# Seven block products for the gate in the up-projection of a two-layer decoder's MLP

## The chip, the cores and the metric

The kernel runs on one core of one Trainium2 chip. The metric is the device time of one execution in microseconds (us). A core has a matrix engine (TensorE, PE in the profile) that multiplies a stationary 128 x 128 block by a moving operand and adds up in PSUM banks of 128 x 512 float32; a vector engine (VectorE, DVE), a scalar engine (ScalarE, ACT), a small general engine (GpSimd, POOL) and a queue that issues transfers (SyncE, SP). Each engine takes its instructions in the order in which they were written into its own queue; engines wait for each other through semaphores.

## What is computed

The reference is a trunk of two layers over 512 positions of width 1024. Each layer has a mixer (windowed attention with a short convolution in layer 0, chunked gated linear attention in layer 1), the gated MLP, and a per-layer embedding. The change is in the MLP, which is the same in both layers:

```
def _conv_ffn(h, w_up, conv_w, conv_b, w_down):
    u = _causal_depthwise_conv(h @ w_up, conv_w) + conv_b
    gate, up = jnp.split(u, 2, axis=-1)
    return (jax.nn.gelu(gate, approximate=False) * up) @ w_down
...
x = x + _conv_ffn(_rms_norm(x, ffn_norm[i]), ffn_w_up[i], ffn_conv_w[i], ffn_conv_b[i], ffn_w_down[i])
```

`h` is 512 x 1024, `w_up` is 1024 x 5632 (2816 gate columns, then 2816 up columns), the convolution goes over three neighbouring positions in each column, and `w_down` is 2816 x 1024. All is float32.

## The kernel before

Activations lie transposed: `xT[k]`, k = 0 to 7, holds 128 features by 512 positions. Every product is made of three matmuls on split operands (`mm3`, lines 157 to 159): a value is its rounded part ("hi", type fp32r) plus the rest ("lo"), and hi x hi, hi x lo and lo x hi are added in one PSUM bank. ACT writes the hi part and DVE subtracts to get the lo part: `split` for activations (lines 101 and 102, with a gain 104 and 105) and `cut` for weights (lines 137 and 138). The RMS norm's factor R, one number per position, is multiplied in after the product (line 785), so `xg[k]` is only the split of `xT[k]` times the norm's gain.

`ffn` (from line 770) goes over 11 column groups. In group d, `weights` loads 256 gate columns and 256 up columns, 1 MB each, into two `raw` buffers (SP's queue, line 111), and cuts each into two hi/lo pairs of 128 x 1024, one per 128-column half. There are three `wh` and three `wl` buffers for these pairs. For each of the two halves PE makes a gate column and an up column, 8 x 3 = 24 matmuls each, 512 positions wide, into a `ps` bank; then `taps` does the rest: z = bank x R on DVE (785), bias and the last tap on ACT (786), the two other taps on DVE (788). The gate column gets Gelu on ACT (810), the product with the up column is formed on DVE (813) and split at once into `acts[f]` (101, 102). There are four `ps` and four `pa` banks, three `z` buffers and four `zt` buffers. The 22 pairs in `acts` are the moving operands of the down-projection, `project` (from line 349), whose three weight chunks per output pair go through the same `raw`, `wh` and `wl` buffers. In layer 1, `blocks` prepares the block sums that the embedding's gate uses, with scratch from the `zt` buffers, and `ple1` takes its transposed rows from there too (`back`).

Which instruction stands where in each queue is not the order of the source. A list scheduler places them by its own costs, except within the stretches marked `manual_schedule`, of which the MLP has none. So matmuls of different columns may be interleaved, and a cut of the next group's weights may stand before or behind the taps of the current one. A tile's buffer is handed on when its last reader is done: the instruction that writes the next tile into it waits for that reader.

Of the kernel before, what the change touches and what calls it, by code (L numbers as in the profile page):

```python
# [18 lines left out]
P = 128  # L19
S = 512  # L20
D = 1024
NT = S // P
ND = D // P
DFF = 2816
NF = DFF // P
# [3 lines left out]
ET = mybir.EngineType  # L29
LEVELS = (64, 32, 16, 8, 4, 2, 1)  # L30
CW = 512
TWO_PI = 2.0 * np.pi
PI_SAFE = 3.1415925

# [22 lines left out]
class Kernel:  # L57
# [60 lines left out]
    def cut(self, rv, by, pool=None, bufs=3):  # L118


        nc = self.nc
        pool = pool or self.wp
        na, nb = rv.shape[1:]
        parts = []
        n = 2 if na * nb > 1024 else 1
        for k in range(n):
            if by == "b":
                a, b = na, nb // n
                v = rv[:, :, k * b : (k + 1) * b]
# [7 lines left out]
            nc.scalar.activation(hv, v, AF.Copy)  # L137
            nc.vector.tensor_tensor(lv, v, hv.bitcast(F32), ALU.subtract)  # L138
# [12 lines left out]
        return get  # L151
# [178 lines left out]
    def spread(self):  # L330
# [7 lines left out]
        for i, x in enumerate((rh.bitcast(F32), rl)):  # L338
# [41 lines left out]
    def rope_tables(self, pool):  # L380
# [54 lines left out]
    def mixer0(self):  # L435
        nc, a, tc = self.nc, self.a, self.tc
        with tc.tile_pool(name="m0", bufs=1) as mp:
# [275 lines left out]
            w = conv_w("x", 0)  # L713
            R = self.spread()
            qn0 = query(0)
# [51 lines left out]
            self.end_norm()  # L767


    def ffn(self, i, next_gain):  # L770
        nc, a, tc = self.nc, self.a, self.tc
        xg, R = self.xg, None
        wu = a["ffn_w_up"][i].rearrange("(k p) n -> p k n", p=P)
        w0, w1, w2, bb = self.fcv
        with tc.tile_pool(name=f"ffn{i}", bufs=1) as fp:
            acts = [self.pair(self.fp, "b0", "b1") for f in range(8)]
            for f in range(8, NF, 2):
                four = self.four(fp)
                acts += [(four[:, 0], four[:, 1]), (four[:, 2], four[:, 3])]

            def taps(ps, f):
                y = fp.tile([P, S], F32, tag="zt", name=self.nm("zt"), bufs=4)
                z = fp.tile([P, S + 2], F32, tag="z", name=self.nm("z"), bufs=3)
                nc.gpsimd.memset(z[:, :2], 0.0)
                nc.vector.tensor_tensor(z[:, 2:], ps, R, ALU.mult)  # L785
                nc.scalar.activation(y, z[:, 2:], AF.Identity, scale=w2[:, f : f + 1], bias=bb[:, f : f + 1])  # L786
                for tap, w in ((1, w1), (0, w0)):
                    nc.vector.scalar_tensor_tensor(  # L788
                        out=y, in0=z[:, tap : tap + S], scalar=w[:, f : f + 1], in1=y, op0=ALU.mult, op1=ALU.add
                    )  # L790
                return y

            for d in range(NF // 2):
                wg = self.weights(wu[:, :, 256 * d : 256 * d + 256], ND, 256)
                wv = self.weights(wu[:, :, DFF + 256 * d : DFF + 256 * d + 256], ND, 256)
                for c in range(2):
                    f = 2 * d + c
                    got = []
                    pss = []
                    for w in (wg, wv):  # L800
                        ps = self.ps()
                        for k in range(ND):
                            self.mm3(ps, w(k, c * P, (c + 1) * P), xg[k], start=k == 0, stop=k == ND - 1)
                        pss.append(ps)
                    if R is None:
                        R = self.spread()
                    for w, ps, fo in ((wg, pss[0], f), (wv, pss[1], NF + f)):
                        y = taps(ps, fo)
                        if w is wg:
                            nc.scalar.activation(y, y, AF.Gelu)  # L810
                        got.append(y)
                    g, y = got
                    nc.vector.tensor_tensor(y, g, y, ALU.mult)  # L813
                    self.split(acts[f], y)
            self.begin_norm(("a0", "a1"))
            done = self.residual(next_gain)
            if i == 1:
                self.forms = []
                scratch = lambda: fp.tile([P, S], F32, tag="zt", name=self.nm("gx"), bufs=4)

                def done(m, ps):
                    nc.vector.tensor_tensor(self.xT[m], self.xT[m], ps, ALU.add)
                    self.blocks(m, next_gain, scratch)
# [75 lines left out]
    def ple1(self, fp):  # L899
# [49 lines left out]
        def back(hf, t):  # L949

            pb = self.pa()
            for q in range(4):
                nc.tensor.transpose(
                    pb[:, q * P : (q + 1) * P], self.xT[4 * hf + q][:, t * P : (t + 1) * P], self.ident
                )
            x = fp.tile([P, 512], F32, tag="zt", name=self.nm("xt"), bufs=4)
            nc.scalar.copy(x, pb)
            return x

# [45 lines left out]
        X, Q = [[self.ps() for _ in range(2)] for _ in range(2)]  # L1005
        both = (0, H)
        with tc.manual_schedule(engines={ET.PE, ET.DVE, ET.Activation}):
# [42 lines left out]
            halves = ((0, H // 2), (H // 2, H))  # L1050
            Y = [Q[0]] + [y[:, : H // 2] for y in (Q[1], X[0])]
# [481 lines left out]
```

## Time and profile before

| what | value |
|---|---|
| median of 3 runs | 1247.51 us (1247.4 to 1247.59) |
| the profiled execution's own time | 1248.2 us |
| its span, first to last instruction | 1246.4 us |
| PE busy | 1236.1 us, 99% of the span |
| DVE busy | 804.6 us, 65% |
| ACT busy | 561.5 us, 45% |
| POOL busy | 52.1 us, 4% |
| granted TensorE clock, mean | 1.0 |
| DMA, mean | 94 GB/s |

The profile is of one execution. Its page names instruction groups by line, engine, operation, written tile and read tiles, then size and count, then busy time and the mean duration in ns of one, then the idle time of the engine before them and what ended most of it. In a timeline each line has the start, the duration, the engine, the line in the source, and in brackets how long the engine had been idle before it and what released it. A line of `mm3`, `split` or `cut` is that of the helper; the tile names (`ps<-a,wh`) tell which product it is. Records of matmuls overlap, since the engine is pipelined.

### The profile page before, as it was taken

What the parts mean: (1) busy time and instruction counts of PE and PEld (TensorE: products, weight loads), DVE (VectorE), ACT (ScalarE), POOL (GpSimd) and SP (SyncE); (2) the same over time, 40 slices, a digit from 0 to 9 for tenths busy, and PEclk for the clock granted to TensorE, in tenths of its full rate; (3) what the DMA queues carried; (4) which work ended last, traced back from release to release, by engine and by line L of the source; (5) the groups of instructions that cost most, each with busy time, mean ns of one, the idle gap of its engine ahead of it and who ended that gap; (6) DMA issues with size and microseconds to landing.
All of it is one profiled execution on the core that took longest, in us unless ns stands there. A gap on an engine that the chain in (4) does not pass through costs nothing.

```text
span 1246.4 us, 15216 instructions
## 1 busy us (share of the span) xinstructions
PE 1236.1 (99%) x5984; PEld 1023.9 (82%) x5984; DVE 804.6 (65%) x1251; ACT 561.5 (45%) x873; POOL 52.1 (4%) x152
## 2 busy tenths in 40 slices
PE   9999999999999999999999999999999999999998
PEld 8877788888888888888987878888888888888887
DVE  6886556777777633346679875557777777444495
ACT  7466344444444322234563554335444444333374
POOL 2500000000000000000100000000000000000000
PEclk9999999999999999999999999999999999999999
DMA  6222232233333232223322222332223333322411
GB/s 214 92 80 56 83 102 83 88 100 102 101 102 101 83 103 93 93 74 103 111 91 68 69 68 68 101 110 95 83 94 102 101 101 102 101 93 94 149 46 68
DMA packets 111004, 117.45 MB, mean 94 GB/s; under 512 B 2728, under 2 KB 106210, under 8 KB 110932
## 3 DMA queue, kind: packets, MB, share of 16 engines
q1 hardware_dynamic: 109568, 115.35, 28.4%
q8 instruction: 47, 0.77, 0.2%
q0 software_dynamic: 560, 0.42, 0.2%
q10 hardware_dynamic: 804, 0.70, 0.2%
q14 instruction: 25, 0.20, 0.0%
HBM read 114.37 MB, written 2.10 MB: 93 GB/s over the span
## 4 chain that ended last, share of the span: by engine, by line
PE 88%; DVE 7%; ACT 2%; issue 1%; POOL 1%; DVEq 0%; ACTq 0%; POOLq 0%
PE ps L157 26%; PE ps L158 26%; PE ps L159 26%; DVE wl L138 1%; PE ps L947 1%; PE ps L946 1%; PE ps L945 1%; PE pa L1367 1%; PE pa L1344 0%; PE pa L595 0%; PE pa L158 0%; PE pa L192 0%; PE pa L159 0%; DVE F L1228 0%; PE pa L157 0%
## 5 line engine op out<-in xcount | busy, mean ns | idle before, releaser
L137 ACT ACTIVATE wh<-raw 128x1024 fp32r<-128x1024 f32 (+4 forms) x212 | 214.2, 1012 | 333.3 <-PE ps L158 298.7
L138 DVE TENSOR_TENSOR wl<-raw,wh 128x1024 fp32r<-128x1024 f32 (+4 forms) x212 | 246.5, 1164 | 153.2 <-ACT wh L137 152.1
L157 PE MATMUL ps<-a,wh 128*128 128x512 f32 x864 | 336.9, 390 | 0.0
L158 PE MATMUL ps<-a,wh 128*128 128x512 f32 x864 | 336.6, 390 | 0.0
L159 PE MATMUL ps<-a,wl 128*128 128x512 f32 x864 | 336.3, 389 | 0.0
L158 PEld LDWEIGHTS ps<-a,wh 128*128 128x128 f32 x864 | 162.3, 188 | 34.0 <-issue 0.3
L159 PEld LDWEIGHTS ps<-a,wl 128*128 128x128 f32 x864 | 162.2, 188 | 33.9
L157 PEld LDWEIGHTS ps<-a,wh 128*128 128x128 f32 x864 | 162.2, 188 | 33.7 <-issue 0.7
L788 DVE SCALAR_TENSOR_TENSOR zt<-z,vfa,zt 128x512 f32<-128x512 f32 x176 | 131.3, 749 | 3.6 <-ACT zt L786 0.6
L157 PE MATMUL ps<-b,wh 128*128 128x512 f32 x320 | 126.0, 395 | 0.5 <-ACT b L101 0.5
L159 PE MATMUL ps<-b,wl 128*128 128x512 f32 x320 | 125.7, 393 | 0.0
L158 PE MATMUL ps<-b,wh 128*128 128x512 f32 x320 | 125.0, 391 | 0.0
L785 DVE TENSOR_TENSOR z<-ps,R 128x512 f32<-128x512 f32 x88 | 60.3, 687 | 74.7 <-PE ps L159 74.7
L157 PE MATMUL ps<-four,wh 128*128 128x512 f32 x224 | 87.1, 389 | 0.0
L158 PE MATMUL ps<-four,wh 128*128 128x512 f32 x224 | 87.1, 389 | 0.0
L159 PE MATMUL ps<-four,wl 128*128 128x512 f32 x224 | 87.1, 389 | 0.0
L786 ACT ACTIVATE zt<-z,vfb 128x512 f32<-128x512 f32 x88 | 70.9, 808 | 5.0 <-DVE z L785 3.3
L157 PEld LDWEIGHTS ps<-b,wh 128*128 128x128 f32 x320 | 60.0, 188 | 14.0 <-ACT b L101 1.3
L159 PEld LDWEIGHTS ps<-b,wl 128*128 128x128 f32 x320 | 60.1, 188 | 12.5
L158 PEld LDWEIGHTS ps<-b,wh 128*128 128x128 f32 x320 | 60.1, 188 | 12.5
L810 ACT ACTIVATE zt<-zt 128x512 f32<-128x512 f32 x44 | 27.8, 631 | 74.9 <-DVE zt L788 74.8
L101 ACT ACTIVATE four<-zt 128x512 fp32r<-128x512 f32 x28 | 17.7, 632 | 77.3 <-DVE zt L813 77.3
(359 smaller groups left out, 1555.0 us busy)
## 6 DMA issues: line engine op xcount, KB each, us to landing
raw<-in_ffn_w_up_dram SPq DMA_DIRECT2D x44, 1024.0 KB, 5.1
raw<-in_ffn_w_down_dram SPq DMA_DIRECT2D x16, 1024.0 KB, 4.7
raw<-in_hy_w_in_dram SPq DMA_DIRECT2D x8, 1024.0 KB, 5.0
raw<-in_gla_w_in_dram SPq DMA_DIRECT2D x8, 1024.0 KB, 5.3
raw<-in_ffn_w_down_dram SPq DMA_DIRECT2D x8, 768.0 KB, 4.1
raw<-in_ple_w_gate_dram SPq DMA_DIRECT2D x6, 1024.0 KB, 4.7
raw<-in_gla_w_out_dram SPq DMA_DIRECT2D x4, 1024.0 KB, 4.8
raw<-in_gla_w_in_dram SPq DMA_DIRECT2D x4, 672.0 KB, 4.0
```

The costliest lines, as they stand in the source:

```text
L101: nc.scalar.activation(h, src, AF.Copy)
L137: nc.scalar.activation(hv, v, AF.Copy)
L138: nc.vector.tensor_tensor(lv, v, hv.bitcast(F32), ALU.subtract)
L157: mm(out, lh, rh, start=start, stop=False)
L158: mm(out, lh, rl, start=False, stop=False)
L159: mm(out, ll, rh, start=False, stop=stop)
L785: nc.vector.tensor_tensor(z[:, 2:], ps, R, ALU.mult)
L786: nc.scalar.activation(y, z[:, 2:], AF.Identity, scale=w2[:, f : f + 1], bias=bb[:, f : f + 1])
L788: nc.vector.scalar_tensor_tensor(out=y, in0=z[:, tap : tap + S], scalar=w[:, f : f + 1], in1=y, op0=ALU.mult, op1=ALU.add)
L810: nc.scalar.activation(y, y, AF.Gelu)
L945: mm(o, lh, rh, start=first and j == 0, stop=False, **kw)
L946: mm(o, lh, rl, start=False, stop=False, **kw)
```

## The change

The activations and weights of a gate group are seen as 2 x 2 blocks: positions left and right (two halves of 256), feature blocks even and odd (`xT[2j]`, `xT[2j+1]`), and columns first and second (two halves of 128). Of the eight block products of such a scheme, seven suffice with sums and differences of blocks (Winograd's form of Strassen's scheme). This is done for the gate in groups d = 2 to 9 of each layer (`SEVEN`); the up columns, and groups 0, 1 and 10, are made as before.

- `sums` makes, from `xT` in groups 0 and 1, the four activation sums of each pair j (four operations of 256 on DVE, two gains on ACT) and splits them (two splits of 512). They lie in the eight `b0`/`b1` pairs, which held the first eight pairs of `acts` before.
- `seven` cuts the first blocks' weights as they are (`w1`), then forms weight differences in place in the `raw` buffer and cuts them: `w13`, `w2` (in the `sq` buffers) and `w4`. It makes seven products of 12 matmuls, 256 positions wide, in three banks W, X and Y; five copies on ACT carry partial results from one half bank to another, and one of them keeps the fourth result, `more`, in SBUF, which `taps` adds to the second column on DVE.
- In the seven-product groups the order in the source is: load of the gate's `raw`, load and cut of the up columns (`wv`), `seven`, `taps` of both gate columns, one Gelu over both (128 x 1024), and then the two up columns, in `pa` banks.
- Results of a group are multiplied in one 128 x 1024 operation and kept unsplit in `kept`; the splits into `acts` come later: the first eight in group 9, the others, two at a time, after the loop in the source.
- `zt` becomes two buffers of 2 x 512 in place of four of 512; `back` in `ple1` and `blocks` take halves of these.

```diff
+    def sums(self, j, gain, scratch):
...
+        for u in range(2):
+            nc.scalar.activation(scratch[:, u], self.xT[2 * j + u], AF.Copy, scale=gain[:, 2 * j + u : 2 * j + u + 1])
+        e, o, s12, s34 = (scratch[:, u] for u in range(4))
+        out = []
+        nc.vector.tensor_tensor(s12[:, :H], e[:, H:], o[:, H:], ALU.add)
+        nc.vector.tensor_tensor(s12[:, H:], s12[:, :H], e[:, :H], ALU.subtract)
+        nc.vector.tensor_tensor(s34[:, :H], e[:, :H], e[:, H:], ALU.subtract)
+        nc.vector.tensor_tensor(s34[:, H:], o[:, :H], s12[:, H:], ALU.subtract)
+        for x in (s12, s34):
+            hl = self.pair(self.fp, "b0", "b1")
+            self.split(hl, x)
...
+    def seven(self, raw, xg, forms):
...
+        W = self.pa()
+        X, Y = self.ps(), self.ps()
+        rv = raw.rearrange("p (j u) n -> p j u n", u=2)
+
+        def cut(src, wide=True):
+
+            if wide:
+                h, l = (self.wp.tile([P, 1024], F32R, tag=g, name=self.nm(g), bufs=3) for g in ("wh", "wl"))
+            else:
+                h, l = (self.sp.tile([P, S], F32R, tag="sq", name=self.nm("t2"), bufs=2) for _ in range(2))
...
+            nc.scalar.activation(h, src, AF.Copy)
+            nc.vector.tensor_tensor(l, src, h.bitcast(F32), ALU.subtract)
...
+        def product(out, w, c, x, first=False):
+            kw = dict(skip_group_check=True)
+            for j in range(ND // 2):
+                (wh, wl), (xh, xl) = w(j, c), x(j)
+                mm(out, wh, xh, start=first and j == 0, stop=False, **kw)
+                mm(out, wh, xl, start=False, stop=False, **kw)
+                mm(out, wl, xh, start=False, stop=j == ND // 2 - 1, **kw)
...
+        w1 = cut(raw[:, :, :P])
+
+        nc.vector.tensor_tensor(b11, b12, b11, ALU.subtract)
+        nc.vector.tensor_tensor(b12, b22, b12, ALU.subtract)
+        w13 = cut(rv[:, :, 0])
+        nc.vector.tensor_tensor(b11, b22, b11, ALU.subtract)
+        w2 = cut(b11, False)
+        nc.vector.tensor_tensor(b21, b21, b11, ALU.subtract)
+        w4 = cut(rv[:, :, 1])
+        product(W[:, left], w1, 0, plain(0, 0), True)
+        nc.scalar.copy(Y[:, left], W[:, left])
+        nc.scalar.copy(X[:, left], W[:, left])
+        product(W[:, right], w13, 0, s1, True)
+        more = self.sp.tile([P, S], F32, tag="acc", name=self.nm("more"), bufs=1)[:, :H]
+        nc.scalar.copy(more, W[:, right])
+        product(Y[:, left], w2, 0, s2)
+        nc.scalar.copy(X[:, right], Y[:, left])
+        product(X[:, left], w1, 1, plain(1, 0))
+        product(X[:, right], w13, 1, s3)
+        nc.scalar.copy(Y[:, right], X[:, right])
+        product(Y[:, left], w4, 1, s4)
+        product(X[:, right], w4, 0, plain(1, 1))
+        return X, Y, more
...
             for d in range(NF // 2):
...
+                g, y = both(), both()
+                cg, cv = 256 * d, DFF + 256 * d
+                if SEVEN[0] <= d < SEVEN[1]:
+                    raw = self.raw(ND, 256)
+                    nc.sync.dma_start(raw, wu[:, :, cg : cg + 256])
+                    wv = self.weights(wu[:, :, cv : cv + 256], ND, 256)
+                    X, Y, more = self.seven(raw, xg, forms)
+                    taps(g[:, 0], X, 2 * d)
+                    taps(g[:, 1], Y, 2 * d + 1, more)
+                    nc.scalar.activation(g, g, AF.Gelu)
+                    for c in range(2):
+                        taps(y[:, c], columns(wv, c, self.pa), NF + 2 * d + c)
+                else:
...
+                nc.vector.tensor_tensor(u, g, y, ALU.mult)
+                if d < 2:
+                    for j in (2 * d, 2 * d + 1):
+                        forms.append(self.sums(j, gain, scratch[j]))
+                if d == SEVEN[1] - 1:
+                    for f in range(8):
+                        hl = self.pair(self.fp, "b0", "b1")
+                        self.split(hl, at(f))
+                        acts.append(hl)
+            for d in range(4, NF // 2):
+                split_pair(y if d == NF // 2 - 1 else kept[d // 2][:, 2 * (d % 2) : 2 * (d % 2) + 2])
```

In the text below, Y left, X right and so on are half banks, a product's number is its place in `seven`, w1, w13, w2, w4 are the cuts above, wv0 and wv1 the two cuts of the up columns, and "bias operation" is the ACT step of `taps` (line 786 before).

More of the change, by code (lines that the diff above doesn't have):

```diff
@@ L31 @@
 CW = 512
+SEVEN = (2, 10)
 TWO_PI = 2.0 * np.pi
@@ L767, in mixer0 @@
             self.end_norm()
+    def sums(self, j, gain, scratch):
+        nc = self.nc
+        H = S // 2
+        for u in range(2):
[9 more added lines that the diff above has]
+            self.split(hl, x)
+            for c in (slice(0, H), slice(H, S)):
+                out.append((hl[0][:, c], hl[1][:, c]))
+        return out
@@ new lines, in seven, with plain @@
+    def seven(self, raw, xg, forms):
+        nc = self.nc
+        H = S // 2
+        mm = nc.tensor.matmul
+        W = self.pa()
[6 more added lines that the diff above has]
+                h, l = (self.sp.tile([P, S], F32R, tag="sq", name=self.nm("t2"), bufs=2) for _ in range(2))
+            h, l = (x.rearrange("p (j n) -> p j n", n=src.shape[2]) for x in (h, l))
+            nc.scalar.activation(h, src, AF.Copy)
+            nc.vector.tensor_tensor(l, src, h.bitcast(F32), ALU.subtract)
+            h, l = (x.rearrange("p j n -> p (j n)").rearrange("p (k n) -> p k n", n=P) for x in (h, l))
+            return lambda j, c: (h[:, (2 * j if wide else j) + c, :], l[:, (2 * j if wide else j) + c, :])
+        def product(out, w, c, x, first=False):
[5 more added lines that the diff above has]
+                mm(out, wl, xh, start=False, stop=j == ND // 2 - 1, **kw)
+        def plain(u, half):
+            c = slice(half * H, (half + 1) * H)
+            return lambda j: (xg[2 * j + u][0][:, c], xg[2 * j + u][1][:, c])
+        s1, s2, s3, s4 = (lambda j, q=q: forms[j][q] for q in range(4))
+        b11, b12, b21, b22 = (rv[:, :, u, c * P : (c + 1) * P] for u in range(2) for c in range(2))
+        left, right = slice(0, H), slice(H, S)
+        w1 = cut(raw[:, :, :P])
[20 more added lines that the diff above has]
+        return X, Y, more
@@ L772, in ffn @@
         xg, R = self.xg, None
+        gain = self.g_ffn[i]
         wu = a["ffn_w_up"][i].rearrange("(k p) n -> p k n", p=P)
@@ L775, in ffn, with both, taps @@
         with tc.tile_pool(name=f"ffn{i}", bufs=1) as fp:
[L776 to L782, printed above, removed]
+            forms, kept, acts = [], [], []
+            def both():
+                return fp.tile([P, 2, S], F32, tag="zt", name=self.nm("zt"), bufs=2)
+            def taps(y, ps, f, more=None):
                 z = fp.tile([P, S + 2], F32, tag="z", name=self.nm("z"), bufs=3)
                 nc.gpsimd.memset(z[:, :2], 0.0)
-                nc.vector.tensor_tensor(z[:, 2:], ps, R, ALU.mult)
+                if more is None:
+                    nc.vector.tensor_tensor(z[:, 2:], ps, R, ALU.mult)
+                else:
+                    h2 = lambda x: x.rearrange("p (u t) -> p u t", u=2)
+                    nc.vector.tensor_tensor(
+                        h2(z[:, 2:]), h2(ps), more.unsqueeze(1).to_broadcast([P, 2, S // 2]), ALU.add
+                    )
+                    nc.vector.tensor_tensor(z[:, 2:], z[:, 2:], R, ALU.mult)
                 nc.scalar.activation(y, z[:, 2:], AF.Identity, scale=w2[:, f : f + 1], bias=bb[:, f : f + 1])
@@ L790, in taps, with columns @@
                     )
-                return y
-            for d in range(NF // 2):
[L794 to L814, printed above, removed]
+            def columns(w, c, bank):
+                ps = bank()
+                for k in range(ND):
+                    self.mm3(ps, w(k, c * P, (c + 1) * P), xg[k], start=k == 0, stop=k == ND - 1)
+                return ps
@@ new lines, in place, with split_pair, at @@
+            def place(d):
+                if d == NF // 2 - 1:
+                    return None
+                if d % 2 == 0:
+                    kept.append(self.four(fp, F32))
+                return kept[d // 2][:, 2 * (d % 2) : 2 * (d % 2) + 2]
+            def split_pair(x):
+                four = self.four(fp)
+                self.split((four[:, :2], four[:, 2:]), x)
+                acts.extend([(four[:, u], four[:, 2 + u]) for u in range(2)])
+            def at(f):
+                return kept[f // 4][:, f % 4]
@@ new lines, in ffn @@
+            scratch = [self.four(fp, F32) for _ in range(ND // 2)]
+            for d in range(NF // 2):
+                g, y = both(), both()
[10 more added lines that the diff above has]
+                        taps(y[:, c], columns(wv, c, self.pa), NF + 2 * d + c)
+                else:
+                    wg = self.weights(wu[:, :, cg : cg + 256], ND, 256)
+                    wv = self.weights(wu[:, :, cv : cv + 256], ND, 256)
+                    for c in range(2):
+                        pss = [columns(w, c, self.ps) for w in (wg, wv)]
+                        if R is None:
+                            R = self.spread()
+                        taps(g[:, c], pss[0], 2 * d + c)
+                        nc.scalar.activation(g[:, c], g[:, c], AF.Gelu)
+                        taps(y[:, c], pss[1], NF + 2 * d + c)
+                u = place(d)
+                if u is None:
+                    u = y
+                nc.vector.tensor_tensor(u, g, y, ALU.mult)
[7 more added lines that the diff above has]
+                        acts.append(hl)
@@ L818, in ffn, with half @@
                 self.forms = []
-                scratch = lambda: fp.tile([P, S], F32, tag="zt", name=self.nm("gx"), bufs=4)
+                halves = []
+                def half():
+                    if not halves:
+                        x = both()
+                        halves.extend([x[:, 0], x[:, 1]])
+                    return halves.pop(0)
+                self.half = half
                 def done(m, ps):
                     nc.vector.tensor_tensor(self.xT[m], self.xT[m], ps, ALU.add)
-                    self.blocks(m, next_gain, scratch)
+                    self.blocks(m, next_gain, half)
             self.project(self.rows(a["ffn_w_down"][i]), acts, ND, done)
@@ L955, in back @@
                 )
-            x = fp.tile([P, 512], F32, tag="zt", name=self.nm("xt"), bufs=4)
+            x = self.half()
             nc.scalar.copy(x, pb)
```

## The prediction

> **What bounds the kernel now.** First the page's busy table and the costliest groups: TensorE (PE) is busy for 99% of the span, and nearly all of that is `mm3`.
>
> ```profile
> PE 1236.1 (99%) x5984; PEld 1023.9 (82%) x5984; DVE 804.6 (65%) x1251; ACT 561.5 (45%) x873; POOL 52.1 (4%) x152
> L157 PE MATMUL ps<-a,wh 128*128 128x512 f32 x864 | 336.9, 390 | 0.0
> L138 DVE TENSOR_TENSOR wl<-raw,wh 128x1024 fp32r<-128x1024 f32 (+4 forms) x212 | 246.5, 1164 | 153.2 <-ACT wh L137 152.1
> L788 DVE SCALAR_TENSOR_TENSOR zt<-z,vfa,zt 128x512 f32<-128x512 f32 x176 | 131.3, 749 | 3.6 <-ACT zt L786 0.6
> L810 ACT ACTIVATE zt<-zt 128x512 f32<-128x512 f32 x44 | 27.8, 631 | 74.9 <-DVE zt L788 74.8
> raw<-in_ffn_w_up_dram SPq DMA_DIRECT2D x44, 1024.0 KB, 5.1
> ```
>
> A mean of 390 ns is a pipelined record, not a price. The price of a matmul is the distance between starts, so I read the timeline of PE twice: 512 wide in a projection, and 256 wide in the key/value product at the start.
>
> ```profile
> 1.32 3.35 PE L192 MATMUL pa<-ones_r 128*128 128x512 f32 x7 [1.32 <-DVE mhalf L181]
> ...
> 8.78 0.28 PE L158 MATMUL pa<-wl,a 128*128 128x256 f32 x1
> 8.90 0.28 PE L159 MATMUL pa<-wh,a 128*128 128x256 f32 x1
> 9.02 0.28 PE L157 MATMUL pa<-wh,a 128*128 128x256 f32 x1
> ...
> 500.13 0.39 PE L158 MATMUL ps<-four,wh 128*128 128x512 f32 x1
> 500.36 0.39 PE L159 MATMUL ps<-four,wl 128*128 128x512 f32 x1
> 500.58 0.39 PE L157 MATMUL ps<-four,wh 128*128 128x512 f32 x1
> ```
>
> 512 columns cost 0.2267 us (three starts span 0.68), 256 columns 0.1196 (0.24 for two): more than half. The first line matters later: seven matmuls out of idle are 0.43 us apart.
>
> Last the timeline of VectorE (DVE) and ScalarE (ACT) inside the MLP, half a column group of the 21.76 us (96 x 0.2267) that one takes:
>
> ```profile
> 310.64 0.69 DVE L102 TENSOR_TENSOR four<-zt,four 128x512 fp32r<-128x512 f32 x1 [0.70 <-ACT four L101]
> 311.25 0.68 DVE L785 TENSOR_TENSOR z<-ps,R 128x512 f32<-128x512 f32 x1
> 311.93 1.23 DVE L138 TENSOR_TENSOR wl<-raw,wh 128x1024 fp32r<-128x1024 f32 x1
> 313.07 1.53 DVE L788 SCALAR_TENSOR_TENSOR zt<-z,vfa,zt 128x512 f32<-128x512 f32 x2
> 316.50 0.69 DVE L785 TENSOR_TENSOR z<-ps,R 128x512 f32<-128x512 f32 x1 [1.90 <-PE ps L159]
> ...
> 310.84 1.06 ACT L137 ACTIVATE wh<-raw 128x1024 fp32r<-128x1024 f32 x1 [0.23 <-PE ps L158]
> 311.97 0.82 ACT L786 ACTIVATE zt<-z,vfb 128x512 f32<-128x512 f32 x1
> ```
>
> Starts on DVE: 0.61 us for 512 elements from SBUF, 0.68 from PSUM, 1.14 for 1024, 0.66 to 0.77 for a tap. On ACT: 1.06 for the hi half of 1024 (0.97 to the next), 0.82 for L786. One engine answers another within 0.04 us (a hi ends at 311.90, its lo starts at 311.93). What the reader is to see: each hi/lo pair is made as soon as PE lets a buffer go. With three buffers and one used up per 24-matmul column (5.44 us), that is two columns, 10.9 us, before PE needs it, and this lead is why PE never waits here.
>
> **The change part by part.** *Matmuls.* A group's gate was 48 at 0.2267 = 10.88 us and becomes 7 x 12 = 84 at 0.1196 = 10.05. The up half stays 10.88. A group is 20.93 us of PE instead of 21.76: 0.83 saved, 16 groups: 13.3 us. That is 7.6% of the gate and not one eighth, because a 256-wide matmul costs 5.5% over half.
>
> *Work on the other engines, per group.* DVE: five lo cuts of 1024 (5.7), one of 512 (0.6), four weight differences of 512 (2.4), five z operations (3.2), eight taps (5.5), one 1024 product (1.1): 18.5 us of 20.9. By the same prices it had 15.2 (four cuts, four z, eight taps, two products, two split halves). ACT gains five half-bank copies from PSUM (`st<-pa`, 256 wide, took 0.376). Neither is full, so neither bounds by volume. The activation splits (22 hi and lo of a layer) only move.
>
> *Order, the dear part.* A group now needs five hi/lo pairs out of the same three buffers: wv0 and wv1 (up half), w1, w13, w4. I follow the three queues as the instructions of the changed kernel stand in them, one group, time 0 at the end of its seventh product, a prime for the next group.
> PE after 0: six matmuls left of the up column (to 1.36), which free wv1's buffer; then at once two of the next group's first product, which need w1' hi, and w1' gets just that buffer. So the lead is gone. On ACT, w1' hi stands behind the bias operations (L786) of both gate columns and of the first up column, the hi of wv0' and wv1', Gelu over 1024, and the bias operation of the second up column. Step by step:
> - z of gate column X on DVE 0.04 to 0.73, its bias operation on ACT to 1.60; four gate taps from 0.91, done 3.71.
> - the load of wv' is issued when w4 lo is cut (2.67 before 0) and lands 5.1 later, at 2.43; hi of wv0' and wv1' then start at 2.47 and 3.44.
> - Gelu 4.41 to about 5.5 (1.1 for 1024, from L810's 0.631 for 512 and L137's two widths).
> - z of the second up column is behind six DVE operations, 4.28 to 4.97; its bias operation waits for Gelu, 5.44 to 6.25; w1' hi 6.17 to 7.23.
> PE waits from 1.36 to 7.27: 5.91 us. It then has 2 x 0.1196 + 8 x 0.2267 = 2.05 of work, until 9.32, and needs w1' lo. DVE reaches that after lo wv0' (5.62), a tap, lo wv1' (7.42) and a tap, 9.22 to 10.45: 1.17 us more. The other handovers (w13, w2, the copies, w4) cost 0.2 together, since the planner put up-column matmuls between them. A group's period is 20.93 + 7.29 = 28.22 us. With 0.10 for each answer instead of 0.04 it is 29.1, with none 27.8.
>
> *Sum.* Seven such boundaries a layer, two layers: 14 x 7.29 = +102.1. The entry into the first of these groups, the last of them (eight splits cut into its queue) and the exit aren't of this form: entry about 1.7 (16 `sums` operations of 256 and 8 splits, 10 to 12 us of DVE, in the second group), last 1.3, exit 1.0, so 4.0 a layer, bounds 0 and 8: +8. Saved: -13.3. Together +96.8.
>
> *PE out of idle.* No gap in the trace of before is over 1.3 us, so it doesn't show what 5.9 us do. Lower bound: nothing. Upper: the nearest row is the start, where matmuls out of idle ran 0.43 apart and the batch of eight at 6.43 still took 2.40 us instead of 1.98 (7 x 0.2267 + 0.39), slow for some 5 us. Five slow microseconds after each gap first stretch the 2.05 us of work to 4.1, of which 1.17 replaces the second wait, then slow part of the next ten: +1.2 a boundary; slow until the next column too, +2.3. I take 0.9: 14 x 0.9 = +12.6.
> [...]
>
> The profiled execution took 1248.2 us (span 1246.4, the rest around it), 0.7 above the median 1247.5. 1248.2 + 96.8 + 12.6 = 1357.6, on the median's footing **1357**.
>
> **The rivals.**
> *The clock stays up.* The same waits, no slow restart: 1247.5 + 96.8 = 1344. For it: the granted clock of the first 2 us window reads 1.00, as everywhere. Against: the starts there are 0.43 apart all the same, so this column does not show such a slowness.
> *Only the buffer turn costs.* ACT would reach w1' hi as soon as PE frees the buffer: 1.06 + 0.1 of wait, lo 1.23 later under 1.8 us of cover, about 1.4 with its smaller handovers. 14 x 1.4 - 13.3 = +6: 1254. Against: both queues are in order, and seven operations stand ahead.
> *Faster.* The matmul saving is kept: 1247.5 - 13.3 = 1234. For it: PE is the bound, 99%, and DVE and ACT have room in volume. It decides where the wait per boundary is under 13.3 / 14 = 0.95 us. Against: the hi cut alone is 1.06 after the buffer comes free, with nothing for PE ahead of it.
> *DVE becomes the bound.* If strided differences and the z sum with a broadcast cost up to twice the 0.61 (at most 5 x 0.61 = 3.1 a group), DVE comes to 21.6 us a group and the late cuts move by up to 3 us: 14 x 3 = 42 on top, 1399. Against: no row has such a stride; taps with one element's offset show no penalty.
>
> **How the numbers follow.** Forecast 0.60, clock stays up 0.20, DVE dearer 0.08, only the buffer turn 0.06, faster 0.06. The first two reach, with periods of 27.8 to 29.1 (14 x -0.4 and +0.9), edges 0 to 8 a layer, and restart 0 to 2.3, from 1330 to 1397. Down to **1305** for waits one third shorter than followed (14 x 2.4 = 34 under 1344 makes 1310, and 4 less if entry, last and exit cost half), and up to **1400**. About 0.15 is left out. One measurement of this kernel tells 0.2% (2.5 us) from no change: faster 0.06, same 0.02 (the tail of the 1254 case), slower 0.92.
>
> **What would show it.** In the changed kernel's page PE's share falls to 91% or so, with waits of the first product's matmul on ACT's `wh` cut, once per group, about 6 us, fourteen times, and a shorter one on DVE's `wl`. The distance of the 256-wide starts should be 0.12. Matmuls behind the long gap should start over 0.4 (512 wide) apart for some microseconds, or the restart term is wrong. Wrong would be: gaps under 1 us at the boundaries, gaps after the second product or after the copies instead, or DVE without idle time in the eight groups.

## The result, and the profile after

| what | before | after |
|---|---|---|
| median | 1247.62 us (6 runs, 1247.4 to 1248.38) | 1364.33 us (6 runs, 1362.66 to 1366.3) |
| profiled execution, span | 1248.2 us, 1246.4 us | 1366.3 us, 1364.5 us |
| up-projection on PE, layer 0 / layer 1 | 240.84 / 240.80 us | 301.64 / 297.28 us |
| granted TensorE clock, mean | 1.0 | 0.966 |

The ratio is 1.0936, with a 95% interval from 1.0922 to 1.095: 116.7 us slower. The up-projection, read as the time from its first matmul to the first of the down-projection, lost 60.8 us in layer 0 and 56.5 in layer 1, together 117.3; so the whole loss lies in the stretch that was changed.

The changed kernel's page, busy table, costliest groups and DMA issues (all helper lines stand one line lower than before):

```profile
PE 1267.4 (93%) x6560; PEld 1058.1 (78%) x6560; DVE 888.5 (65%) x1375; ACT 617.3 (45%) x987; POOL 52.6 (4%) x152
L139 DVE TENSOR_TENSOR wl<-raw,wh 128x1024 fp32r<-128x1024 f32 (+4 forms) x180 | 206.9, 1151 | 141.4 <-ACT wh L138 141.4
L879 DVE SCALAR_TENSOR_TENSOR zt<-z,vfa,zt 128x512 f32<-128x512 f32 x176 | 124.9, 746 | 10.2 <-ACT zt L877 9.9
L818 PE MATMUL pa<-a,wh 128*128 128x256 f32 x64 | 24.8, 387 | 85.7 <-ACT wh L809 85.7
raw<-in_ffn_w_up_dram SPq DMA_DIRECT2D x44, 1024.0 KB, 5.0
```

PE now idles 85.7 us ahead of one group of 64 matmuls: L818 is the first matmul of a product, and what it waits for is the hi cut of `w1` on ACT (L809). The price of a tap (746 ns, was 749) and of a weight cut's lo half (1151 ns, was 1164) hardly changed. PE is busy for more microseconds than before (1267 against 1236) although it has less to multiply: slow matmuls count as busy.

One boundary between two seven-product groups, in the timeline of PE:

```profile
318.28 0.58 PE L818 MATMUL pa<-a,wh 128*128 128x256 f32 x1 [5.68 <-ACT wh L809]
318.65 0.42 PE L819 MATMUL pa<-a,wh 128*128 128x256 f32 x1
318.87 0.63 PE L158 MATMUL pa<-a,wh 128*128 128x512 f32 x1
319.30 0.63 PE L159 MATMUL pa<-a,wh 128*128 128x512 f32 x1
...
321.43 0.44 PE L158 MATMUL pa<-a,wh 128*128 128x512 f32 x1
321.71 0.39 PE L159 MATMUL pa<-a,wh 128*128 128x512 f32 x1
321.94 0.28 PE L820 MATMUL pa<-a,wl 128*128 128x256 f32 x1
```

The same boundary on ACT:

```profile
311.34 2.23 ACT L877 ACTIVATE zt<-z,vfb 128x512 f32<-128x512 f32 x3 [3.43 <-DVE z L876]
313.62 2.00 ACT L138 ACTIVATE wh<-raw 128x1024 fp32r<-128x1024 f32 x2
315.53 1.04 ACT L916 ACTIVATE zt<-zt 128x1024 f32<-128x1024 f32 x1
316.48 0.80 ACT L877 ACTIVATE zt<-z,vfb 128x512 f32<-128x512 f32 x1
317.18 1.04 ACT L809 ACTIVATE wh<-raw 128x1024 fp32r<-128x1024 f32 x1
```

This is the queue that the prediction followed: three bias operations, both hi cuts of wv', Gelu, a fourth bias operation, and only then `w1'`. PE had stopped at 312.60 (318.28 - 5.68), when the last up column ended; that buffer was free from then on, and ACT reached it 4.6 us later. After the gap the matmuls are 0.43 us apart, and from 321.71 on 0.23 again.

The table by stretches of the same boundary (us; busy time and instructions of PE, PEld, DVE, ACT and POOL; granted clock; DMA share; GB/s):

```profile
316.00:318.20 2.20, 0.00 (x0) 0.00 (x0) 2.20 (x4) 2.20 (x3) 0.10 (x1) 0.50 0.00 0
318.30:319.30 1.00, 1.00 (x4) 0.91 (x4) 1.00 (x2) 0.00 (x0) 0.00 (x0) 0.50 0.00 0
322.30:325.00 2.70, 2.70 (x18) 2.36 (x17) 1.78 (x3) 0.64 (x2) 0.00 (x0) 1.00 0.74 259
```

In the last 2.2 us of PE's wait DVE and ACT work without a pause: over the span they have time to spare (DVE 65%), but too much to do just here. The granted clock is already 0.50 in the gap and stays there for the first matmuls behind it.

### The profile page after: what moved, and what is told of

Same layout as the page of the kernel before. It is cut to its first block, busy times and chain, and to the rows that moved or that the text cites. A ratio compares the mean times of both kernels' runs of the same rounds, so it can differ in the third digit from the quotient of the medians.

```text
span 1364.5 us, 16685 instructions
## 1 busy us (share of the span) xinstructions
PE 1267.4 (93%) x6560; PEld 1058.1 (78%) x6560; DVE 888.5 (65%) x1375; ACT 617.3 (45%) x987; POOL 52.6 (4%) x152
## 4 chain that ended last, share of the span: by engine, by line
PE 74%; DVE 11%; ACT 9%; issue 2%; DMA 2%; POOL 1%; DVEq 0%; POOLq 0%; ACTq 0%
PE ps L158 14%; PE ps L159 14%; PE ps L160 14%; PE pa L158 5%; PE pa L159 5%; PE pa L160 4%; ACT wh L138 2%; DMA raw<-in_ffn_w_up_dram 2%; ACT zt L877 2%; PE ps L818 2%; PE pa L818 2%; PE ps L820 2%; PE ps L819 2%; ACT wh L809 2%; DVE wl L139 1%
## 5 line engine op out<-in xcount | busy, mean ns | idle before, releaser
L138 ACT ACTIVATE wh<-raw 128x1024 fp32r<-128x1024 f32 (+4 forms) x180 | 178.3, 1000 | 303.2 <-PE ps L159 253.8
L139 DVE TENSOR_TENSOR wl<-raw,wh 128x1024 fp32r<-128x1024 f32 (+4 forms) x180 | 206.9, 1151 | 141.4 <-ACT wh L138 141.4
L158 PE MATMUL ps<-a,wh 128*128 128x512 f32 x352 | 138.0, 392 | 0.9 <-ACT wh L138 0.9
L159 PE MATMUL ps<-a,wh 128*128 128x512 f32 x352 | 137.4, 390 | 0.0
L160 PE MATMUL ps<-a,wl 128*128 128x512 f32 x352 | 137.4, 390 | 0.0
L158 PE MATMUL pa<-a,wh 128*128 128x512 f32 x256 | 109.8, 429 | 0.0
L159 PE MATMUL pa<-a,wh 128*128 128x512 f32 x256 | 109.5, 428 | 0.0
L160 PE MATMUL pa<-a,wl 128*128 128x512 f32 x256 | 106.8, 417 | 0.0
L810 DVE TENSOR_TENSOR wl<-raw,wh 128x1024 fp32r<-128x1024 f32 x48 | 58.7, 1222 | 70.2 <-ACT wh L809 70.2
L818 PE MATMUL pa<-a,wh 128*128 128x256 f32 x64 | 24.8, 387 | 85.7 <-ACT wh L809 85.7
L818 PEld LDWEIGHTS pa<-a,wh 128*128 128x128 f32 x64 | 16.2, 254 | 93.6 <-ACT wh L809 92.5
L158 PEld LDWEIGHTS ps<-a,wh 128*128 128x128 f32 x352 | 66.1, 188 | 15.7 <-ACT wh L138 1.7
L809 ACT ACTIVATE wh<-raw 128x1024 fp32r<-128x1024 f32 x48 | 50.6, 1054 | 60.1 <-PE ps L819 23.5
L160 PEld LDWEIGHTS ps<-a,wl 128*128 128x128 f32 x352 | 66.1, 188 | 14.5 <-DVE wl L139 0.8
```

The costliest lines, as they stand in the source:

```text
L158: mm(out, lh, rh, start=start, stop=False)
L159: mm(out, lh, rl, start=False, stop=False)
L160: mm(out, ll, rh, start=False, stop=stop)
L809: nc.scalar.activation(h, src, AF.Copy)
L810: nc.vector.tensor_tensor(l, src, h.bitcast(F32), ALU.subtract)
L818: mm(out, wh, xh, start=first and j == 0, stop=False, **kw)
```

## The experiments

All medians stand beside runs of the kernel before on the same chip; ratios are to those, with 95% intervals.

| run | what it is | us | ratio |
|---|---|---|---|
| late_split | only the late splits, no seven-product group | 1250.05 | 1.0017 [1.0008, 1.0026] |
| one_group | one seven-product group per layer | 1254.51 | 1.0052 [1.0037, 1.0067] |
| warm | filler matmuls in the gap | 1360.94 | 1.0905 [1.0889, 1.0922] |
| prep_first | next group's loads and w1 cut ahead of the taps | 1325.62 | 1.0621 [1.0603, 1.0639] |
| own_w1 | own buffer for the w1 pair | 1338.36 | 1.0727 [1.0711, 1.0743] |
| own_prep | both of these | 1256.68 | 1.0071 [1.0056, 1.0086] |
| roomy | and own raw buffers for the up columns | 1252.41 | 1.0033 [1.002, 1.0045] |
| edges | and both ends of the stretch prepared ahead | 1253.03 | 1.0045 [1.0031, 1.0059] |
| lazy | and the last splits where they are first needed | 1243.78 | 0.9968 [0.9956, 0.998] |

**Is it the boundaries, or the rest of the change?** Two kernels take boundaries out and leave the rest.

```diff
-SEVEN = (2, 10)
+SEVEN = (10, 10)      (late_split)
+SEVEN = (9, 10)       (one_group)
```

> No group is made with seven products; the activation sums are still formed in groups 0 and 1 (their results go unused), the activations are split late and zt is two wide buffers, as in the changed kernel. Theory (the loss sits in the handover of weight buffers between seven-product groups): at most the entry, sums and late splits, 1247 to 1256 us. Rival (late splitting or the sums carry a good part of the 117 us): 1275 us or more.

> Only group 9 of each layer is made with seven products, so there is no boundary between two of them. Theory: entry and exit only, 2 x (1.5 to 5) less 2 x 0.83, 1249 to 1257 us. Rival (each seven-product group costs by itself, through its products, copies or differences, 117 / 16 = 7.3 us): 1247.6 + late_split's loss + 14.6, about 1265 us.

late_split came 2.1 us over before (1250.05 against 1247.96): the moved splits, the block sums, the wider product and the new buffers cost nearly nothing alone. One group per layer, which has an entry and an exit but no boundary between two such groups, adds 4.5 us. So some 110 of the 117 us belong to the boundaries.

**How dear is the slow restart?** The same kernel, with 22 matmuls on a tile of ones in each boundary's gap, so that PE never stops for long; the order of the other work is held.

```diff
+        if after is not None:
+            rhs = self.ones_r.unsqueeze(1).to_broadcast([P, NT, P])
+            with self.tc.issue_after(after.ins):
+                for _ in range(22):
+                    mm(W, self.ones_r, rhs, start=True, stop=True, skip_group_check=True)
```

> All queues stand as in the changed kernel, with 22 matmuls of ones (512 wide, result overwritten) added on PE in each of the 14 long waits, about 5.0 of the 5.4 to 6.9 us, so that PE never idles long. Theory: the granted clock stays at 1.0, matmuls behind the wait are 0.227 apart at once, the wait for w1' lo of about 1.2 us shows itself, and a boundary gets some 1.0 us shorter: 1350 us (1342 to 1356). If the slow restart were worth all of the 2.3 us by which the matmuls behind a gap are late: 1332. If the clock did not matter: 1364.

It came out at 1360.94: only 3.4 us less than after where 14 were expected (1350), and above the expected range. The waits of PE in it, two boundaries:

```profile
348.36 0.39 PE L818 MATMUL pa<-a,wh 128*128 128x256 f32 x1 [0.53 <-ACT wh L809]
351.94 0.39 PE L822 MATMUL pa<-a,wl 128*128 128x256 f32 x1 [1.24 <-DVE wl L810]
377.15 0.39 PE L818 MATMUL pa<-a,wh 128*128 128x256 f32 x1 [0.53 <-ACT wh L809]
380.74 0.39 PE L822 MATMUL pa<-a,wl 128*128 128x256 f32 x1 [1.24 <-DVE wl L810]
```

With matmuls at full speed (0.39 records) the second wait, on the lo cut of `w1'`, is there as forecast: 1.24 us (forecast 1.17). In after the slow matmuls cover it. Boundaries 2 to 7, from one group's first matmul to the next one's, take 174.20 us in layer 0 and 173.20 in layer 1; in after they take 181.46 and 176.68. That is 1.21 and 0.58 us per boundary, 0.9 on the mean, the forecast's term. The total gained less because the first boundary is longer in warm, 31.1 us against 27.6, in each layer: in after the planner had put 18 up-column matmuls where the order held here allows 8, and in warm PE waits 1.92 us there for the lo cut, and 512-wide matmuls soon behind it start 0.43 us apart (236.23 to 238.79 in layer 0). The experiment was therefore not as clean as meant; the comparison of boundaries 2 to 7 is the part that answers. It bundles everything that the filler changed there, the late loads (below) too: in layer 0 ACT waits for four of them in after and for two in warm, in layer 1 for none in after and one in warm. So layer 1's 0.58 is nearer to the clock alone than layer 0's 1.21, and that the mean is just 0.9 is partly luck.

**Place in the queue, or buffer?** prep_first changes the place alone, own_w1 the buffer alone, own_prep both.

```diff
+                    raw, wv, first = ready or prep(d)                       (prep_first, own_prep)
+                    X, Y, more = self.seven(raw, xg, forms, first)
+                    pss = [columns(wv, c, self.pa) for c in range(2)]
+                    ready = prep(d + 1) if d + 1 < SEVEN[1] else None
...
-                h, l = (self.wp.tile([P, 1024], F32R, tag=g, name=self.nm(g), bufs=3) for g in ("wh", "wl"))
+                four = self.four(fp)                                        (own_w1, own_prep; w1 only)
+                h, l = (four[:, 2 * u : 2 * u + 2].rearrange("p a b -> p (a b)") for u in range(2))
```

`prep(d)` issues the loads of group d and traces the cuts of `w1` and of the up columns; it now stands ahead of the taps and Gelu of group d - 1.

> The same work with the same buffers as the changed kernel; only the source order differs: loads and first cut (w1) of the next group are traced ahead of the taps of this one, the first cut ahead of the up cuts. In the queues w1' now stands before the sixth product and the up cuts behind three taps. [...] Rival (the seven products or their volume on DVE are what costs): over 1340 us.

> The changed kernel in its own source order, but the hi/lo pair of a group's first weight block (w1) gets a buffer of its own, so that it no longer takes the buffer which up column c1 frees last. Theory (the place in the queue ties the cut, the buffer is only the second tie): with the buffer free, the planner can put the w1' cut ahead of the taps in some boundaries, and in these the long wait is gone and a shorter one, on the hi of wv0', of 1 to 3 us, takes its place; where it still stands behind the bias operations and Gelu, the wait of 5 to 6 us stays. In the instruction order of this kernel about every second boundary is of the early kind, so about half of the boundary loss of 108 us goes: 1290 to 1325 us. Rival 1 (the buffer alone is the tie): all long waits go, 1250 to 1275. Rival 2 (volume of work on VectorE paces a group): no change, 1355 to 1370.

> The kernel with the next group's loads and w1 cut ahead of the taps (prep_first, 1325.6 us), and the w1 pair in a buffer of its own. Now four pairs a group go through the three buffers instead of five, and the load of the up columns still waits for a raw buffer that the cut of w4 frees. Theory: the wait on w1' stays gone; the one on the hi of wv0' (2.96 us per boundary in prep_first, set by a load issued late) stays in part, at 1 to 3 us, and the shorter ones go: 14 x (1 to 3) + the handovers inside a group, which eat the 13 saved, + 3 to 5 for the slow matmuls: 1265 to 1310. Rival (work on VectorE paces a group): about 1325, as without the buffer.

Against after, the place alone gains 38.7 us, the buffer alone 26.0, both together 107.6. Neither tie was the cause alone: with one loosened, the other holds. Views of waits and of a timeline show this. In prep_first, the longest of PE's waits:

```profile
PE pa L158 <- ACT wh L138: 32.9, 30, 2.8
PE pa L820 <- ACT wh L798: 7.3, 12, 0.6
```

The columns are total, times and longest. The long wait on `w1'` is gone (7.3 us in 12 times); in its place PE waits for the hi of wv0' (L138), because five pairs still go through three buffers and the load is issued late. ACT's line there:

```profile
333.79 2.01 ACT L138 ACTIVATE wh<-raw 128x1024 fp32r<-128x1024 f32 x2 [0.77 <-DMA raw<-in_ffn_w_up_dram]
```

Expected were 1275 to 1295: the time of before plus 14 waits of 3.0 and 8 for the ends, less 13.3, with no slow restart. This wait and the half clock (below) are why 1325.62 is above that: the direction was right, the next tie was undersized, and waits of 1.92 to 2.80 us brought slow matmuls (512-wide starts 0.43 apart), for which the estimate had nothing. In own_w1, all of PE's waits on that cut:

```profile
PE pa L821 <- ACT four L812: 47.9, 8, 8.6
```

Eight of the 14 boundaries kept a wait, 5.12 us in most; the other six have none over 0.9 us. The planner cut two groups' `w1` one behind the other, behind Gelu and the bias operations, in every second boundary. So nearly half the boundaries were freed, as expected, but the time is above the expected 1290 to 1325: behind each of the eight waits follows one of 1.44 us on the lo half, and in layer 1 matmuls start 0.43 us (512 wide) or 0.21 (256 wide) apart until 7.5 to 9.2 us after the longer of the two waits ended. With a free buffer and an unchanged place in ACT's queue the full wait remains, which rules out the rival that only the buffer turn costs. own_prep, at 1256.68, is better than the 1265 expected: with four pairs a group the wait on wv0' went too. ACT still waits for that load (1.73 us at the boundary at 315 us), but PE has matmuls to do meanwhile. DVE does the same 1375 operations in it as in after, so their volume isn't the bound.

**What is left without boundary waits?** roomy takes the last tie, the load.

```diff
+                rawv = self.four(fp, F32).rearrange("p a b -> p (a b)").rearrange("p (a b) -> p a b", b=256)
+                nc.sync.dma_start(rawv, wu[:, :, cv : cv + 256])
+                wv = self.cut(rawv, "b")
```

> As own_prep, and the raw buffers of the up columns apart too, so that each load is out a whole group ahead: neither queue place, nor pair buffer, nor load ties the next group. Theory (waits at the boundaries are of order, buffers and loads; in-group handovers cost about 0.8 us a group, so the saving of 13.3 us is eaten, and the later splits and block sums cost 2.5 to 4 us): few waits over 1 us are left and the time is 1248 to 1268 us. Rival 1 (VectorE's volume paces a group): 1300 or more, with VectorE hardly idle. Rival 2 (a matmul behind a handover costs nothing of its own): the saving shows, 1236 to 1246.

1252.41, as expected. In the whole up-projection of layer 0, PE waits four times:

```profile
230.81 0.39 PE L824 MATMUL pa<-a,four 128*128 128x256 f32 x1 [0.68 <-DVE four L801]
234.41 0.49 PE L160 MATMUL pa<-a,wl 128*128 128x512 f32 x1 [1.21 <-DVE wl L139]
410.50 0.50 PE L158 MATMUL ps<-a,wh 128*128 128x512 f32 x1 [0.65 <-ACT wh L138]
412.13 0.50 PE L160 MATMUL ps<-a,wl 128*128 128x512 f32 x1 [0.89 <-DVE wl L139]
```

All four are at the ends: two where the stretch is entered, two where group 10 follows it. Adding up by how much each start is later than 0.2267 or 0.1196 us behind the one before gives 8.6 us of lateness per layer, against 6.65 saved (8 x 0.83).

**The ends.**

```diff
-                    ready = prep(d + 1) if d + 1 < SEVEN[1] else None
+                    ready = prep(d + 1) if d + 1 < SEVEN[1] else self.weights(wu[:, :, cg + 256 : cg + 512], ND, 256)
...
+                        if c == 1 and d + 1 == SEVEN[0]:
+                            ready = prep(d + 1)
```

> As roomy (1252.4 us), with the two ends of the stretch prepared ahead as the groups inside it are: the first seven-product group's loads and w1 cut are traced ahead of the taps and block sums of group 1, and the gate weights of group 10 ahead of the taps and the eight splits of group 9. Theory: in roomy the waits that are left are at the entry (0.6 + 1.4 us of late starts per layer, lo halves on VectorE) and at the exit (0.8 + 1.1); without them 2 x 3.9 = 7.8 us go, of which the taps and sums moved behind may give back 1 to 2: 1243 to 1248 us, for the first time not slower than before, by up to 0.4%. Inside the groups about 0.5 us of late starts behind handovers stays, so that of the saved 13.3 us some 8 are not had. Rival (the waits at the ends move to the next handover): 1250 to 1254.

The rival won: 1253.03. The up-projection became shorter than before for the first time (238.91 us in layer 0), and the wait came back in the down-projection. PE, then DVE, in edges:

```profile
423.76 0.39 PE L159 MATMUL ps<-b,wh 128*128 128x512 f32 x1
427.16 0.79 PE L160 MATMUL ps<-b,wl 128*128 128x512 f32 x1 [3.01 <-DVE wl L139]
```

```profile
422.36 1.22 DVE L103 TENSOR_TENSOR four<-four,four 128x1024 fp32r<-128x1024 f32 x1
423.49 0.68 DVE L872 TENSOR_TENSOR z<-ps,R 128x512 f32<-128x512 f32 x1
424.09 1.21 DVE L103 TENSOR_TENSOR four<-four,four 128x1024 fp32r<-128x1024 f32 x1
425.23 0.74 DVE L881 SCALAR_TENSOR_TENSOR zt<-z,vfa,zt 128x512 f32<-128x512 f32 x1
425.89 1.22 DVE L139 TENSOR_TENSOR wl<-raw,wh 128x1024 fp32r<-128x1024 f32 x1
```

The lo cut that PE needs at 423.99 stands behind splits (L103) of activations that the down-projection reads only in its second weight chunk. The last kernel traces each of these splits where it is first read:

```diff
-            for d in range(4, NF // 2):
-                split_pair(y if d == NF // 2 - 1 else kept[d // 2][:, 2 * (d % 2) : 2 * (d % 2) + 2])
+            class Lazy(list):
...
+                def __getitem__(self, f):
+                    if f >= 8 and f not in self.done:
+                        e = f // 2
+                        split_pair(y if e == NF // 2 - 1 else kept[e // 2][:, 2 * (e % 2) : 2 * (e % 2) + 2])
...
-            self.project(self.rows(a["ffn_w_down"][i]), acts, ND, done)
+            self.project(self.rows(a["ffn_w_down"][i]), later, ND, done)
```

> As edges (1253.0 us), but the splits of the last 14 activations are traced one pair at a time where the down-projection first needs them, so that the lo cuts of its first two weight pairs stand ahead of three of these splits in VectorE's queue. In edges the up-projection stage was 238.9 us, for the first time shorter than the 240.8 of before, but the down-projection then waited 3.01 us for a lo cut behind the splits, with slow matmuls behind it, 3.2 to 4.2 us of late starts per layer. Theory: that wait is the whole of what keeps edges above before; without it 6.4 to 8.4 us go: 1243 to 1247.5 us, 0.1 to 0.4% under before. Rival (the splits are late for the second weight chunk instead, and the wait comes there): 1249 to 1254.

1243.78 us, ratio 0.9968 [0.9956, 0.998]: 4.25 us faster than before, with the seven products in place. Of the 13.3 us saved in matmuls, two thirds are still lost, though no wait over 0.15 us is shown in the whole stretch. Where they go is seen in PE's and ACT's timelines of lazy:

```profile
311.00 0.39 PE L159 MATMUL pa<-a,wh 128*128 128x512 f32 x1
311.30 0.39 PE L822 MATMUL ps<-b,wh 128*128 128x256 f32 x1
311.52 0.28 PE L823 MATMUL ps<-b,wh 128*128 128x256 f32 x1
311.64 0.27 PE L824 MATMUL ps<-b,wl 128*128 128x256 f32 x1
311.75 0.28 PE L822 MATMUL ps<-b,wh 128*128 128x256 f32 x1
```

```profile
310.88 0.36 ACT L851 COPY ps<-ps 128x256 f32<-128x256 f32 x1
```

Starts should be 0.2267 behind a 512-wide and 0.1196 behind a 256-wide matmul. Instead 311.00 to 311.30 is 0.07 too long and 311.30 to 311.52 0.10: the product needs a bank that ACT's copy finished at 311.24, just in time. No idle time is shown, since the record of a matmul (0.39) runs 0.16 past the next start and covers the gap. The change of width is not the cause: 37 of 50 256-wide matmuls behind a 512-wide one in layer 0 of this trace start less than 0.01 late. Late starts sum to 4.75 us per layer, about 0.6 per group; 6.65 - 4.75 = 1.9 saved per layer, 3.8 in both, and 4.25 was measured.

## Why the prediction was right

1357 us were forecast, 1364.33 measured, by the mechanism that was forecast. Per layer, in us; the measured periods run from one group's first matmul to the next one's, less the 21.76 that a group took before:

| piece | forecast | layer 0 | layer 1 |
|---|---|---|---|
| seven boundaries, 7 x (7.29 + 0.9 - 0.83) | 51.5 | 56.7 | 51.9 |
| entry, last group and exit, less its 0.83 | 3.2 | 4.1 | 4.6 |

- **Matmul prices.** Right: full-speed starts in the changed kernel are 0.12 (256 wide) and 0.23 (512 wide) apart, as in the lazy lines above. The 13.3 us are really saved, as lazy shows by beating the kernel before.
- **Order of the queues.** Right, operation by operation. With time 0 at 311.24 (1.36 before PE stopped), wv0' hi starts at 2.38 (forecast 2.47), Gelu at 4.29 (4.41), `w1'` hi at 5.94 (6.17). The idle time before it is 5.51 us in six of layer 1's boundaries, where 5.91 was forecast.
- **Second wait and restart.** The second wait (forecast 1.17) isn't seen in after, where the late starts behind the gap come to 1.6 to 2.9 us, 2.3 on the mean; forecast was 1.17 + 0.9 = 2.07 for both. The 0.9 was the author's choice between bounds of 0 and 2.3, and no run shows it as a term of its own: warm shows the wait again at 1.24, and in place of the 0.9 a net 0.58 in layer 1, where after has no late load, and 1.21 in layer 0, where it has four. The rival in which the clock stays up falls: 0.50 is granted behind the gap. So the granted clock does show the slowness; the 1.00 of the first 2 us, from which the prediction doubted it, stands where the trace has no clock record yet (the first of before begins at 7.11 us).
- **Other handovers.** Undersized: 0.2 forecast, 0.5 to 0.6 measured per group, in late starts of about 0.1 and less that show no idle time. In layer 1 about half of the difference is offset by the shorter first wait.
- **The loads.** This is the step that makes most of the 7 us of difference, 5.0 us of idle time: "the load of wv' is issued when w4 lo is cut ... and lands 5.1 later". In layer 1 it holds, and ACT waits for it at no boundary. In layer 0's later boundaries ACT waits, and every step behind it, `w1'` too, comes later: idle times of 6.5 to 6.9 us, and 56.7 us against 51.9 in all. In after, on ACT:

```profile
373.95 2.00 ACT L138 ACTIVATE wh<-raw 128x1024 fp32r<-128x1024 f32 x2 [1.22 <-DMA raw<-in_ffn_w_up_dram]
```

  That load was issued at 367.47 and released ACT 6.5 us later. The row of the page (5.0, a median) hides it. The DMA records of the trace set the four late loads of layer 0 apart: in each, a transfer of 16 KB on the instruction queue (q8 of the page) starts 0.1 to 1.6 us behind the load's first packet. Here it runs from 369.73 to 371.04, the load's packets from 368.52 to 373.58. No other load of `w_up` in that trace has one starting there. That the one slows the other is likely but not shown: no run takes these transfers away.
- **Entry, last, exit.** 4.1 and 4.6 against 3.2, and the wait at the entry is 1.3 and 1.4 us. But a measured period ends where the next group starts, so the late starts behind the seventh gap (2.2 and 2.5 us) fall into this row. Put where the forecast has them, the boundaries took 58.9 and 54.4 us against 51.5, and the ends 1.9 and 2.1 against 3.2. The sum is thus nearer than its parts, which is partly luck.
- **PE's share.** 93% instead of 91%: the slow matmuls count as busy, which the forecast of the share left out.
- **The other rivals.** Only the buffer turn (1254): own_w1 has the buffer free and still waits 5.12 us. DVE dearer (1399): the strided differences and the sum with a broadcast take 683 to 692 ns, as the contiguous operations of 512 do (0.69), and own_prep does all of DVE's work in 1256.68. Faster (1234): its test, a wait per boundary under 0.95 us, is needed but not enough. roomy has no wait at a boundary between two groups and is 4.4 us slower than before, for its ends and handovers. lazy has no such wait at the ends either and is faster, but by 4.25 and not 13.3, for the handovers, which the rival had at nothing.

## What to carry to other kernels

A change that saves work on the engine that bounds can be lost many times over if it uses up the lead with which the others prepare that engine's operands. Count the buffers that a step turns over, find the one that the next step's first operand takes, and read what stands ahead of its writer in the writer's queue. Both ties have to be loosened: here the place alone gave 39 us, the buffer alone 26, both 108; and the wait then moved on to the load, the ends and the next stage, until no operand was late.

## What the runs showed of the hardware that was not expected

- The half clock can come after the wait, when PE is at work again. In prep_first PE waited 2.80 us, started at 334.90 and ran 512-wide matmuls at the granted clock of 1.00 until 336.3; then it fell. The table by stretches of prep_first:

```profile
334.80:336.30 1.50, 1.18 (x4) 0.71 (x5) 1.42 (x2) 1.50 (x3) 0.00 (x0) 1.00 0.02 5
336.60:339.80 3.20, 3.20 (x9) 2.50 (x9) 3.20 (x5) 2.10 (x4) 0.10 (x1) 0.51 0.42 126
340.00:342.00 2.00, 2.00 (x10) 1.61 (x9) 1.81 (x3) 0.01 (x1) 0.17 (x2) 0.98 0.80 283
```

  Nor does the length of the wait alone decide. In layer 0 of prep_first slow matmuls (512-wide starts 0.43 apart) followed waits of 2.47 to 2.80 us and one of 1.92 (ended at 280.09), but not the other of 1.92 (at 361.35) or that of 1.45; in edges they followed the 3.01 us of layer 0. In after the granted clock is 0.50 from 256.67 to 263.50, from 287.39 to 294.22 and from 314.70 to 321.52, each time for 6.8 us, with starts 30.72 and 27.31 apart. What decides the time of the change these runs do not show.
- In after, the granted clock stayed at 0.50 for 3.2 to 6.2 us behind a gap (1021.47 to 1024.67 and 288.00 to 294.22). The length of the gap doesn't set this: both extremes followed gaps of 5.51 us.
- A matmul that was released just in time cost 0.17 us in the case shown (0.07 on its own start, 0.10 on the next), and no view of waits shows it. Before, the starts of a whole up-projection are late by less than 0.1 us in sum; in lazy by 4.75.
